# The attention output and the first token tile of the delta output turned by VectorE's blocks and a way through DRAM, in an encoder kernel of two layers

## The chip, the cores and the metric

The kernel runs on one core of one Trainium2 chip. The metric is the device time of one execution in microseconds (us), and the number compared is a median of runs. A core has a matrix engine (TensorE, PE in the profile), a vector engine (VectorE, DVE), a scalar engine (ScalarE, ACT), a general engine (GpSimd, POOL) and a sync engine (SyncE, SP) that here only issues transfers. Each works through its own queue of instructions in order, and instructions of different engines wait for one another by semaphores. PE writes its results into PSUM; the other engines bring them from there to SBUF. DMA engines move data between SBUF and DRAM.

## What is computed

Two layers of an encoder over 256 tokens with 1024 channels, in float32. Each layer projects its normalised input into the parts of two branches (a gated delta rule in both directions, and differential attention), gates the output of each branch, projects both, merges them and projects the result. The parts of the reference that matter here:

```python
def gated_delta_branch(q, k, v, ab, z, conv_w, a_log, dt_bias, norm_w):
    ...
    o = rmsnorm(o_fwd + o_bwd, norm_w.astype(f32))
    o = o.transpose(0, 2, 1, 3).reshape(bsz, seq, GDN_WIDTH).astype(z.dtype)
    return o * jax.nn.silu(z)

def diff_attention_branch(q, k, v, z, cos, sin, lam_params, subln_w, lambda_init):
    ...
    o = rmsnorm(o, subln_w) * (1.0 - lambda_init)
    o = o.transpose(0, 2, 1, 3).reshape(bsz, seq, DIFF_WIDTH)
    return o * jax.nn.silu(z)

    for l in range(DEPTH):
        h = rmsnorm(x, norm_w[l])
        proj = h @ w_in[l]
        ...
        y_a = gated_delta_branch(q_a, k_a, v_a, ab_a, z_a, ...)
        y_b = diff_attention_branch(q_b, k_b, v_b, z_b, ...)
        merged = (jax.nn.sigmoid(gate_a) * (y_a @ w_pa[l])
                  + jax.nn.sigmoid(gate_b) * (y_b @ w_pb[l]))
        x = x + merged @ w_out[l]
```

To multiply `y_a` and `y_b` by their weights, PE needs them with channels on the partitions, while they are made with tokens on the partitions. The change is about how they are turned.

## The kernel before

The 256 tokens are two tiles of 128 (m=0 and m=1), and the 1024 channels of an output are two halves of 512 (i=0 and 1), each of four heads of 128. Float32 values are multiplied as a high and a low part: for each pair of operands PE makes the products high by high (L286), high by low (L287) and low by high (L288). A token-major projection of one half (`proj_tm`) is 48 products of 128x512: eight slices `kt` of the 1024 inputs, two token tiles, three products.

The weights come in four pairs of slices per half (`weights`). Each pair is loaded by SP into `raw_*`, cast to its high part by ACT (L270, `hi_*`) and subtracted to its low part by DVE (L272, `lo_*`). `hi_*` and `lo_*` have two buffers each, so the cast of a pair waits until PE is through with the pair two before it. A name such as `lo_pb011` is layer 0, half 1, pair 1 of projection `pb`; `pp_pb000` is the PSUM bank of half 0, token tile 0.

At the end of a layer the projections run in this order: `gb` and `ga` (the two merge gates), `pb` (attention output by its weights), `pa` (delta output by its weights), then the merge (`mg`) and the output projection `o`. The output of a `pb` product is brought from PSUM by DVE with the gate (L1102). In between, the delta rule is finished by chunk stages (`chunks`, for the two groups of four heads): `y1p`, `sp`, `ks`, `y2p` and `qs`, and `po`, of 128x128 products on PE, copies on ACT and additions on DVE (the last of them L921, onto `kq`, where the delta output lies). A list of places says behind which slice of which projection each stage is issued: places 48 to 55 are the slices of `ga` half 0, 56 to 63 of `ga` half 1, 64 to 71 of `pb` half 0. A scheduler then sets the order of each engine's queue.

When the delta output is complete, ACT squares its 16 rows of heads (L1155, into `sso`), DVE and POOL make the factor `ro` (L1157, POOL's power at L157, L1159), and DVE multiplies by the factor and by the gate `za` (L1080, eight instructions for each token tile). The attention output `ob` is gated in the same way with `zb` earlier, about the time of the second half of `gb` and the first of `ga`.

The gated tiles are turned by `split_T`: four PE turns of 128x128 into a PSUM bank (L213, `pt_yb*` and `pt_ya*`), from which ACT writes the high part, scaled by the norm's weight (L222), and DVE the low part (L223) into `ybT` or `yaT`. There are four such sets of turns for each output and layer: two halves by two token tiles.

Another tile of the kernel is turned without PE already: `v` and the squares of `q` go through DVE's 32x32 block turns (L136, `tb_v`, `tb_q`), and `v` goes by POOL into a DRAM tile (L141, `bnc_v`) and back in four pieces that put the blocks in their places (L143).

## Time and profile before

| | |
|---|---|
| median of 3 runs | 758.26 us (757.37 to 758.40) |
| profiled execution | 758.15 us |
| its span, first to last instruction | 756.4 us |
| granted TensorE clock | 0.998 of full speed |
| PE, DVE, ACT, POOL busy, share of the span | 99%, 77%, 62%, 16% |
| PE turns per layer of `yb` and of `ya` | 16 and 16 |
| idle of PE put down to `lo_pa` | 0.5 us, once |

A page of the profile shows one execution on the chip. A row of a group names the line of the code, the engine, the operation, the tiles as out<-in, and then count, busy time and the idle time ahead of it with what ended it. A row of a timeline starts with its start and its duration in us; "x4" at its end joins four instructions, and square brackets hold the idle time before the first and the engine and line that ended it. PE's products overlap, so that the distance between two starts, not the duration, is what one costs. Times in the text are us in the span of the profiled execution.

### The profile page before, as it was taken

The page shows a single profiled execution, that of the slowest core. Times are in us where ns is not written, and L with a number is a line of the kernel's source. Part 1 is how long each engine was busy: PE and PEld are TensorE (multiplying, and loading weights), DVE is VectorE, ACT ScalarE, POOL GpSimd, SP SyncE. Part 2 cuts the span into 40 slices and gives each one's busy share as a digit, 9 for nine tenths or more (in the row PEclk, how much of TensorE's full clock was granted, in tenths as well). Part 3 has the DMA queues.
Part 4 walks back from the last instruction along what each step waited for, and adds up shares of the span by engine and source line. Part 5 has one row for each costly group of instructions (what it writes and reads, how often), then busy time and mean ns, then how long its engine had stood idle before and what let it go on. Part 6 is the DMA issues. An engine that isn't in the chain of part 4 may idle for free.

```text
span 756.4 us, 13840 instructions
## 1 busy us (share of the span) xinstructions
PE 745.5 (99%) x5192; PEld 642.2 (85%) x5192; DVE 581.0 (77%) x1098; ACT 471.8 (62%) x1015; POOL 121.0 (16%) x181
## 2 busy tenths in 40 slices
PE   8999999999999999999999999999999999999996
PEld 5999889977878889988889889889788888998785
DVE  7786999999886853578668779999998668436782
ACT  6657665568876675645445677565787747465552
POOL 5101431112032030100000025202111310201000
PEclk9999999999999999999999999999999999999999
DMA  8752767776677342567574258768665835336541
GB/s 261 232 167 83 229 194 206 215 217 175 202 191 178 85 120 84 168 203 240 196 230 140 84 148 258 203 187 238 181 185 183 190 114 143 104 110 207 194 140 56
DMA packets 71811, 131.26 MB, mean 174 GB/s; under 512 B 12303, under 2 KB 12767, under 8 KB 71744
## 3 DMA queue, kind: packets, MB, share of 16 engines
q1 hardware_dynamic: 64606, 113.65, 50.6%
q0 software_dynamic: 6304, 15.15, 7.5%
q10 hardware_dynamic: 834, 1.58, 0.6%
q8 instruction: 41, 0.67, 0.4%
q14 instruction: 26, 0.21, 0.1%
HBM read 123.44 MB, written 6.91 MB: 172 GB/s over the span
## 4 chain that ended last, share of the span: by engine, by line
PE 86%; DVE 7%; issue 3%; DMA 2%; ACT 2%; POOL 0%; POOLq 0%; DVEq 0%; ACTq 0%
PE pp_vb L344 4%; PE pp_qk L287 3%; PE pp_qk L288 3%; PE pp_qk L286 3%; PE pf_v L361 2%; PE pp_za L287 2%; PE pp_gb L287 2%; PE pf_v L365 2%; PE pp_gb L286 2%; PE pf_v L363 2%; PE pp_ga L286 2%; PE pp_za L286 2%; PE sc L955 2%; PE pp_za L288 2%; PE pp_gb L288 2%
## 5 line engine op out<-in xcount | busy, mean ns | idle before, releaser
L287 PE MATMUL pp_qk<-lo_qk,hT 128*128 128x512 f32 x128 | 50.9, 398 | 0.4 <-DVE lo_qk L272 0.2
L288 PE MATMUL pp_qk<-hi_qk,hT 128*128 128x512 f32 x128 | 50.0, 391 | 0.0
L272 DVE TENSOR_TENSOR lo_qk<-raw_qk,hi_qk 128x1024 fp32r<-128x1024 f32 x32 | 39.8, 1242 | 9.7 <-ACT hi_qk L270 9.3
L270 ACT CAST hi_qk<-raw_qk 128x1024 fp32r<-128x1024 f32 x28 | 29.4, 1050 | 25.3 <-PE pp_qk L288 12.6
L286 PE MATMUL pp_qk<-hi_qk,hT 128*128 128x512 f32 x128 | 45.1, 393 | 0.0
L965 ACT ACTIVATE es<-sc,mx 128x256 f32<-128x256 f32 x64 | 29.6, 473 | 19.6 <-DVE mx L963 19.6
L272 DVE TENSOR_TENSOR lo_pb<-raw_pb,hi_pb 128x1024 fp32r<-128x1024 f32 x16 | 19.6, 1226 | 23.0 <-ACT hi_pb L270 23.0
L363 PE MATMUL pf_q<-hT,hi_q 128*128 128x256 f32 x128 | 36.2, 286 | 0.0
L361 PE MATMUL pf_q<-hT,hi_q 128*128 128x256 f32 x128 | 36.1, 287 | 0.0
L361 PE MATMUL pf_v<-hT,hi_v 128*128 128x256 f32 x128 | 35.9, 285 | 0.0
L363 PE MATMUL pf_v<-hT,hi_v 128*128 128x256 f32 x128 | 35.8, 284 | 0.0
L361 PE MATMUL pf_k<-hT,hi_k 128*128 128x256 f32 x128 | 35.7, 284 | 0.0
L363 PE MATMUL pf_k<-hT,hi_k 128*128 128x256 f32 x128 | 35.7, 283 | 0.0
L272 DVE TENSOR_TENSOR lo_ga<-raw_ga,hi_ga 128x1024 fp32r<-128x1024 f32 x16 | 19.5, 1219 | 20.9 <-ACT hi_ga L270 20.9
L365 PE MATMUL pf_q<-hT,lo_q 128*128 128x256 f32 x128 | 34.8, 285 | 0.0
L365 PE MATMUL pf_v<-hT,lo_v 128*128 128x256 f32 x128 | 34.6, 288 | 0.0
L365 PE MATMUL pf_k<-hT,lo_k 128*128 128x256 f32 x128 | 34.4, 284 | 0.0
L593 DVE SCALAR_TENSOR_TENSOR cvq<-pf_q,cw,cvq 128x254 f32<-128x254 f32 (+1 forms) x64 | 29.9, 476 | 1.9 <-ACT cvq L589 1.4
L270 ACT CAST hi_pa<-raw_pa 128x1024 fp32r<-128x1024 f32 x16 | 16.8, 1053 | 22.9 <-PE pp_pa L288 16.7
L287 PEld LDWEIGHTS pp_qk<-lo_qk,hT 128*128 128x128 f32 x128 | 24.0, 188 | 7.3 <-DVE lo_qk L272 2.5
L593 DVE SCALAR_TENSOR_TENSOR cvv<-pf_v,cw,cvv 128x254 f32<-128x254 f32 (+1 forms) x64 | 30.0, 476 | 0.1
L593 DVE SCALAR_TENSOR_TENSOR cvk<-pf_k,cw,cvk 128x254 f32<-128x254 f32 (+1 forms) x64 | 28.5, 478 | 2.0 <-ACT cvk L589 1.3
(392 smaller groups left out, 2524.1 us busy)
## 6 DMA issues: line engine op xcount, KB each, us to landing
raw_qk<-in_w_in_dram SPq DMA_DIRECT2D x32, 512.0 KB, 4.0
raw_k<-in_w_in_dram SPq DMA_DIRECT2D x16, 512.0 KB, 5.3
raw_q<-in_w_in_dram SPq DMA_DIRECT2D x16, 512.0 KB, 3.7
raw_v<-in_w_in_dram SPq DMA_DIRECT2D x16, 512.0 KB, 3.8
raw_zb<-in_w_in_dram SPq DMA_DIRECT2D x16, 512.0 KB, 3.8
raw_za<-in_w_in_dram SPq DMA_DIRECT2D x16, 512.0 KB, 3.8
raw_ga<-in_w_in_dram SPq DMA_DIRECT2D x16, 512.0 KB, 4.2
raw_pb<-in_w_pb_dram SPq DMA_DIRECT2D x16, 512.0 KB, 3.8
```

Of the source, the lines that this page charges most:

```text
L270: high = (V.tensor_copy if kp in turned else S.copy)(hi[:, :, :n], raw[:, :, :n]).ins
L272: mark[nm, kp] = high, V.tensor_tensor(lo[:, :, :n], raw[:, :, :n], hi[:, :, :n].bitcast(F32), ALU.subtract).ins
L286: T.matmul(o, act[kt // 4][:, 0, kt % 4, ts_], hi, start=kt == 0, stop=False)
L287: T.matmul(o, act[kt // 4][:, 0, kt % 4, ts_], lo, start=False, stop=False)
L288: mark["proj"] = T.matmul(o, act[kt // 4][:, 1, kt % 4, ts_], hi, start=False, stop=kt == KT - 1).ins
L344: mark["proj"] = T.matmul(o, act[k_ // 4][:, pa, k_ % 4, ts_], ws[k_][1 + pw], start=k_ == 0 and n_ == 0, stop=kt == KT - 1 and n_ == len( ...
L361: T.matmul(o, hi[:, cs], act[kt // 4][:, 0, kt % 4, :], start=first, stop=False, skip_group_check=True)
L363: T.matmul(o, hi[:, cs], act[kt // 4][:, 1, kt % 4, :], start=False, stop=False, skip_group_check=True)
L365: T.matmul(o, lo[:, cs], act[kt // 4][:, 0, kt % 4, :], start=False, stop=done, skip_group_check=True)
L593: V.scalar_tensor_tensor(ca[:, o0:o1], acc[:, b, o0 + sft : o1 + sft], cw[:, j, cb : cb + 1], ca[:, o0:o1], ALU.mult, ALU.add)
L955: mm = T.matmul(sp[n][:, qt * SEQ : (qt + 1) * SEQ], qkT[h // 4][rows, 0, h % 4, qt * P : (qt + 1) * P], qkT[h // 4][rows, 1, h % 4, :], s ...
L965: S.activation(es[:, n, qt, :], spv[:, qt, :], AF.Exp, bias=mx[:, n, qt : qt + 1], accum_out=s_all[:, h, n, qt : qt + 1])
```

## The change

In the gated attention output, all four tiles of a layer, and in the gated delta output, the two tiles of m=0, the four PE turns are replaced. `send` turns a gated tile by 32x32 blocks on DVE into the buffer of the gate that it was multiplied by (`zb` or `za`), and POOL writes it to a DRAM tile `bny`. `fetch` has POOL read it back in four pieces of 64 KB, in which the blocks stand at their places. `split_B` lets ACT make the high part and DVE the low part from that buffer in SBUF, behind a named weight pair. The delta output's m=1 stays with `split_T`. The places of the chunk stages are moved from 52, 54, 57, 59, 62, 64, 67 to 52, 54, 55, 57, 58, 60, 61. Weights, products and all other stages are as before.

```diff
--- before.py
+++ after.py
@@ -221,6 +221,27 @@
         else:
             S.activation(hi, ptv, AF.Copy, scale=w)
             V.scalar_tensor_tensor(lo, ptv, w, hi.bitcast(F32), ALU.mult, ALU.subtract)
+
+    def send(tb, src, nm):
+
+        V.transpose(tb.rearrange("p j (d k) -> p j k d", k=4), src.rearrange("p k (j t) -> p j k t", j=4))
+        dd = dram.tile([4, 32, 4, P], F32, tag="bny", name=f"bny_{nm}", bufs=4)
+        mark["sent"] = G.dma_start(out=dd.rearrange("i t j x -> (i t) (j x)"),
+                                   in_=tb.rearrange("p j x -> p (j x)")).ins
+        return dd
+
+    def fetch(tb, dd, after):
+        for j in range(4):
+            with behind(after):
+                G.dma_start(out=tb[blk(j)], in_=dd[:, :, j].rearrange("i t x -> t i x"))
+
+    def split_B(dst, tb, m, w, after):
+        turned = tb.rearrange("p i (d k) -> p k (i d)", k=4)
+        hi, lo = (dst[:, part, :, m * P : (m + 1) * P] for part in range(2))
+        with behind(after[0]):
+            S.activation(hi, turned, AF.Copy, scale=w)
+        with behind(after[1]):
+            V.scalar_tensor_tensor(lo, turned, w, hi.bitcast(F32), ALU.mult, ALU.subtract)
 
     def pair(nm):
         return [big.tile([P, 2, 4, SEQ], F32R, tag="p8", name=f"{nm}_{i}", bufs=4) for i in range(2)]
@@ -1071,7 +1092,7 @@
         step(mg)
         step(mg)
 
-        def gated(o_, z_, r_, nw_, yT, nm, tiles=range(NM), after={}, halves_=range(2)):
+        def gated(o_, z_, r_, nw_, yT, nm, tiles=range(NM), after={}, halves_=range(2), sent=None):
             for i in halves_:
                 for m in tiles:
                     zv, ov = heads4(z_[i][:, m, :]), o_(i, m)
@@ -1080,7 +1101,11 @@
                             V.scalar_tensor_tensor(ov[:, j, :], ov[:, j, :],
                                                    r_[:, m, 4 * i + j : 4 * i + j + 1],
                                                    zv[:, j, :], ALU.mult, ALU.mult)
-                    split_T(yT[i], ov, m, f"{nm}{i}", w=nw_)
+                    if sent is None:
+                        split_T(yT[i], ov, m, f"{nm}{i}", w=nw_)
+                    else:
+                        tb = z_[i][:, m, :].rearrange("p (j x) -> p j x", j=4)
+                        sent[i, m] = tb, send(tb, ov, f"{nm}{i}{m}")
 
         def gate(c_base, nm, tag, between=(None, None), places=((None,) * 4,) * 2, first=(),
                  raws=({}, {})):
@@ -1117,14 +1142,18 @@
         rsqrt_rows(rb.rearrange("p q h -> p (q h)"), ssb.rearrange("p q h -> p (q h)"), 1.0 / P, 16)
         V.scalar_tensor_tensor(rb, rb, 0.5 * (1.0 - lam0), r0, ALU.mult, ALU.mult)
 
-        ybT = pair(f"ybT{l}")
+        ybT, yb_sent = pair(f"ybT{l}"), {}
         def gate_yb(i):
             at = [mark[f"ga{l}0", m][1] if i else mark[f"gb{l}1", 2 + m][1] for m in range(NM)]
             gated(lambda i, m: heads4(ob[i][:, m, :]), zb, rb, nw[:, 1:2], ybT, f"yb{l}",
-                  after={(i, m): at[m] for m in range(NM)}, halves_=(i,))
+                  after={(i, m): at[m] for m in range(NM)}, halves_=(i,), sent=yb_sent)
+            for m in range(NM):
+                fetch(*yb_sent[i, m], None)
 
         gate_yb(0)
         gta = gate(C_GA, f"ga{l}", "eo", (lambda: gate_yb(1), None))
+        for i, m in ((0, 0), (0, 1), (1, 0), (1, 1)):
+            split_B(ybT[i], yb_sent[i, m][0], m, nw[:, 1:2], mark[f"ga{l}{i}", 2 + m])
         branch(ybT, w_pb[l], gtb, f"pb{l}")
         ch = [chunks(0), chunks(1)]
 
@@ -1134,7 +1163,7 @@
                 next(gen, None)
 
         order = [(mg, 41), (mg[:1], 43), (mg[1:], 45), (mg, 48), (mg, 50)]
-        order += [(ch[i : i + 1], at + i) for at in (52, 54, 57, 59, 62, 64, 67) for i in range(2)]
+        order += [(ch[i : i + 1], at + i) for at in (52, 54, 55, 57, 58, 60, 61) for i in range(2)]
         for gens, at in order:
             if at == 52:
                 key_sums()
@@ -1149,7 +1178,7 @@
         V.tensor_tensor(rq2, rq, rq, ALU.mult)
         sso = small.tile([P, NM, NH], F32, tag="sso", name=f"sso{l}")
         ro = small.tile([P, NM, NH], F32, tag="ro", name=f"ro{l}")
-        yaT = pair(f"yaT{l}")
+        yaT, ya_sent = pair(f"yaT{l}"), {}
         for m in range(NM):
             for h in range(NH):
                 S.activation(sqj[:, :P], osb(h // 4, m)[:, h % 4, :], AF.Square,
@@ -1157,7 +1186,11 @@
             V.tensor_tensor(sso[:, m], sso[:, m], rq2[:, m], ALU.mult)
             rsqrt_rows(ro[:, m], sso[:, m], 1.0 / P, NH)
             V.scalar_tensor_tensor(ro[:, m], ro[:, m], 0.5, rq[:, m], ALU.mult, ALU.mult)
-            gated(osb, za, ro, nw[:, 0:1], yaT, f"ya{l}", (m,))
+            gated(osb, za, ro, nw[:, 0:1], yaT, f"ya{l}", (m,), sent=None if m else ya_sent)
+        for i in range(2):
+            fetch(*ya_sent[i, 0], mark["pow"])
+        for i in range(2):
+            split_B(yaT[i], ya_sent[i, 0][0], 0, nw[:, 0:1], mark[f"pb{l}1", 2 + i])
         branch(yaT, w_pa[l], gta, f"pa{l}")
 
 
```

In the changed kernel lines stand 21 further down from L225 on, and some more behind `gated`: L270 and L272 become L291 and L293, L286 to L288 become L307 to L309, L921 becomes L942, L1080 becomes L1101, L1102 becomes L1127, and L1155, L1157 and L1159 become L1184, L1186 and L1188. New are L227 (the block turn), L229 and L236 (the DMAs), L242 and L244 (`split_B`).

DVE's queue in layer 0, from the first weight pair of `pb`'s second half (`lo_pb010`) on; first before, then with the change:

```order
L1080 SCALAR_TENSOR_TENSOR kq0_344<-kq0_344,ro0_3680,za0_1_372 128x128 x4
L272 TENSOR_TENSOR lo_pb010_3133<-raw_pb010_3134,hi_pb010_3132 128x1024
L1102 SCALAR_TENSOR_TENSOR gb0_0_2743<-gb0_0_2743,pp_pb000_3054 128x512
L1157 TENSOR_TENSOR sso0_3679<-sso0_3679,rq20_3674 128x8
L1102 SCALAR_TENSOR_TENSOR gb0_0_2743<-gb0_0_2743,pp_pb001_3055 128x512
L272 TENSOR_TENSOR lo_pb011_3151<-raw_pb011_3152,hi_pb011_3150 128x1024
L223 SCALAR_TENSOR_TENSOR yaT0_0_3681<-pt_ya000_3700,nw0_291,yaT0_0_3681 128x4x128
```

```order
L293 TENSOR_TENSOR lo_pb010_3141<-raw_pb010_3142,hi_pb010_3140 128x1024
L1127 SCALAR_TENSOR_TENSOR gb0_0_2743<-gb0_0_2743,pp_pb000_3062 128x512
L1188 SCALAR_TENSOR_TENSOR ro0_3688<-ro0_3688,rq0_3683 128x8
L1127 SCALAR_TENSOR_TENSOR gb0_0_2743<-gb0_0_2743,pp_pb001_3063 128x512
L1186 TENSOR_TENSOR sso0_3687<-sso0_3687,rq20_3682 128x8
L1101 SCALAR_TENSOR_TENSOR kq0_344<-kq0_344,ro0_3688,za0_0_371 128x128 x4
L1101 SCALAR_TENSOR_TENSOR kq0_344<-kq0_344,ro0_3688,za0_1_372 128x128 x4
L293 TENSOR_TENSOR lo_pb011_3159<-raw_pb011_3160,hi_pb011_3158 128x1024
L227 STREAM_TRANSPOSE za0_0_371<-kq0_344 128x4x4x32
L1188 SCALAR_TENSOR_TENSOR ro0_3688<-ro0_3688,rq0_3683 128x8
L227 STREAM_TRANSPOSE za0_1_372<-kq0_344 128x4x4x32
L293 TENSOR_TENSOR lo_pb012_3177<-raw_pb012_3178,hi_pb012_3176 128x1024
```

The eight multiplies by the gate of m=0 (on `kq0_344`, with `za0`) stood ahead of `lo_pb010` and now stand between `lo_pb010` and `lo_pb011`, and the first block turn follows `lo_pb011`.

ACT's queue in layer 0, from the last weight pair of `pb`; before, then with the change:

```order
L270 CAST hi_pb013_3186<-raw_pb013_3188 128x1024
L222 ACTIVATE yaT0_0_3681<-pt_ya001_3735,nw0_291 128x4x128
L222 ACTIVATE yaT0_1_3682<-pt_ya011_3746,nw0_291 128x4x128
L270 CAST hi_pa000_3755<-raw_pa000_3757 128x1024
L270 CAST hi_pa001_3773<-raw_pa001_3775 128x1024
L270 CAST hi_pa002_3791<-raw_pa002_3793 128x1024
```

```order
L291 CAST hi_pb013_3194<-raw_pb013_3196 128x1024
L291 CAST hi_pa000_3767<-raw_pa000_3769 128x1024
L222 ACTIVATE yaT0_0_3689<-pt_ya001_3735,nw0_291 128x4x128
L222 ACTIVATE yaT0_1_3690<-pt_ya011_3746,nw0_291 128x4x128
L291 CAST hi_pa001_3785<-raw_pa001_3787 128x1024
L242 ACTIVATE yaT0_0_3689<-za0_0_371,nw0_291 128x4x128
L242 ACTIVATE yaT0_1_3690<-za0_1_372,nw0_291 128x4x128
L291 CAST hi_pa002_3803<-raw_pa002_3805 128x1024
```

The high parts of the turned m=0 (L242, from `za0`) stand behind the cast of the second weight pair of `pa`; L222 is now for m=1 alone.

PE's queue in layer 0, from the last product of `pb`; before, then with the change:

```order
L288 MATMUL pp_pb011_3131<-hi_pb013_3186,ybT0_1_2855 128x512
L286 MATMUL pp_pa000_3753<-hi_pa000_3755,yaT0_0_3681 128x512
L286 MATMUL pp_pa001_3754<-hi_pa000_3755,yaT0_0_3681 128x512
L287 MATMUL pp_pa000_3753<-lo_pa000_3756,yaT0_0_3681 128x512
L288 MATMUL pp_pa000_3753<-hi_pa000_3755,yaT0_0_3681 128x512
L287 MATMUL pp_pa001_3754<-lo_pa000_3756,yaT0_0_3681 128x512
L288 MATMUL pp_pa001_3754<-hi_pa000_3755,yaT0_0_3681 128x512
```

```order
L309 MATMUL pp_pb011_3139<-hi_pb013_3194,ybT0_1_2855 128x512
L307 MATMUL pp_pa000_3765<-hi_pa000_3767,yaT0_0_3689 128x512
L308 MATMUL pp_pa000_3765<-lo_pa000_3768,yaT0_0_3689 128x512
L307 MATMUL pp_pa001_3766<-hi_pa000_3767,yaT0_0_3689 128x512
L308 MATMUL pp_pa001_3766<-lo_pa000_3768,yaT0_0_3689 128x512
L309 MATMUL pp_pa001_3766<-hi_pa000_3767,yaT0_0_3689 128x512
L307 MATMUL pp_pa001_3766<-hi_pa000_3767,yaT0_0_3689 128x512
L308 MATMUL pp_pa001_3766<-lo_pa000_3768,yaT0_0_3689 128x512
L309 MATMUL pp_pa001_3766<-hi_pa000_3767,yaT0_0_3689 128x512
L307 MATMUL pp_pa001_3766<-hi_pa001_3785,yaT0_0_3689 128x512
L308 MATMUL pp_pa001_3766<-lo_pa001_3786,yaT0_0_3689 128x512
L309 MATMUL pp_pa001_3766<-hi_pa001_3785,yaT0_0_3689 128x512
```

The bank of m=0 is `pp_pa000`, that of m=1 `pp_pa001`. Both before and now the first product is of m=0; then came products of both tiles by turns, and now ten and more products of m=1 follow, up to the second weight pair, ahead of the return to m=0 (`pp_pa000` with `hi_pa000`).

## The prediction

> **What bounds the kernel now.** I read the page first: span, busy shares, the shares of the chain.
>
> ```profile
> span 756.4 us, 13840 instructions
> PE 745.5 (99%) x5192; PEld 642.2 (85%) x5192; DVE 581.0 (77%) x1098; ACT 471.8 (62%) x1015; POOL 121.0 (16%) x181
> PE 86%; DVE 7%; issue 3%; DMA 2%; ACT 2%; POOL 0%; POOLq 0%; DVEq 0%; ACTq 0%
> ```
>
> TensorE is busy for 745.5 of 756.4 us. Next I asked for busy time in two stretches of layer 0 (columns: PE, its weight loads, DVE, ACT, POOL, clock, DMA share, GB/s), from the attention output's first turns to the delta output's, and from there to the first product of `pa`.
>
> ```profile
> 256.25:320.45 64.20, 64.20 (x514) 57.46 (x513) 35.97 (x66) 40.25 (x93) 7.59 (x8) 1.00 0.42 129
> 320.45:333.18 12.73, 12.73 (x65) 10.63 (x64) 11.02 (x21) 6.54 (x8) 1.83 (x2) 1.00 0.62 205
> ```
>
> In both PE has no idle time and its clock is 1.00: a product taken off PE is time gained, unless the work that replaces it comes late. But in the second stretch DVE is busy for 11.02 of 12.73 us, so whatever is put there has almost no room.
>
> **What the change takes from PE.** Six sets of four 128x128 turns a layer leave PE: four of the attention output, two of the delta output's tile m=0. One set, between products:
>
> ```profile
> 270.31 0.60 PE L213 MATMUL pt_yb<-ident,ob 128*128 128x128 f32 x4
> 270.67 0.48 PE L287 MATMUL pp_ga<-lo_ga,hT 128*128 128x512 f32 x1
> 270.98 0.39 PE L288 MATMUL pp_ga<-hi_ga,hT 128*128 128x512 f32 x1
> 271.21 0.40 PE L287 MATMUL pp_ga<-lo_ga,hT 128*128 128x512 f32 x1
> ```
>
> A set holds PE from 270.31 to 270.67, 0.36 us; the product behind it takes 0.31 to the next start where the one after takes 0.23, 0.08 more. So 0.44 a set, 2.7 for six. The chunk stages' small products, which now stand in fewer and longer blocks, save some changes of form: two or three of the 0.08, about 0.2. Gain: 2.9 a layer, 5.8 in all.
>
> **Cost a: the weights of `pb`, second half, behind the gating on DVE.** In the order of before, only the two evacuations of `gb` stand between the low parts of the weight pairs 0 and 1 of `pb010`/`pb011`; the eight gating multiplies of m=0 were done earlier. Now the four additions of `po` end together, all squares wait for the last of them, so the gating comes late, between these two subtractions. Rows of DVE and ACT as they are now:
>
> ```profile
> 305.49 0.69 DVE L921 TENSOR_TENSOR kq<-po,kq 128x512 f32<-128x512 f32 x1 [1.46 <-PE po L919]
> 320.19 0.68 DVE L1102 SCALAR_TENSOR_TENSOR gb<-gb,pp_pb 128x512 f32<-128x512 f32 x1
> 320.79 0.16 DVE L1157 TENSOR_TENSOR sso<-sso,rq 128x8 f32<-128x8 f32 x1
> 320.87 0.68 DVE L1102 SCALAR_TENSOR_TENSOR gb<-gb,pp_pb 128x512 f32<-128x512 f32 x1
> 321.74 1.23 DVE L272 TENSOR_TENSOR lo_pb<-raw_pb,hi_pb 128x1024 fp32r<-128x1024 f32 x1 [0.19 <-ACT hi_pb L270]
> 324.21 0.15 DVE L1159 SCALAR_TENSOR_TENSOR ro<-ro,rq 128x8 f32<-128x8 f32 x1
> 324.40 2.19 DVE L1080 SCALAR_TENSOR_TENSOR kq<-kq,ro,za 128x128 f32<-128x128 f32 x8
> 308.04 0.30 ACT L1155 ACTIVATE sqj<-kq 128x128 f32<-128x128 f32 x1
> 308.46 0.31 ACT L1155 ACTIVATE sqj<-kq 128x128 f32<-128x128 f32 x1
> 308.90 0.31 ACT L1155 ACTIVATE sqj<-kq 128x128 f32<-128x128 f32 x1
> 311.74 1.03 ACT L270 CAST hi_pb<-raw_pb 128x1024 fp32r<-128x1024 f32 x1
> 322.73 0.40 PE L286 MATMUL pp_pb<-hi_pb,ybT 128*128 128x512 f32 x1
> 326.59 0.40 PE L288 MATMUL pp_pb<-hi_pb,ybT 128*128 128x512 f32 x1
> ```
>
> The two PE rows are 17 products apart: 3.86/17 = 0.227 a product, 2.73 for the 12 of a weight pair. Call E the end of the last `po` block, two products into half 0. Additions: four steps of about 0.6 (DVE's small overlap taken off its 0.69), the first result 0.35 ahead of E, so E+2.05. Squares, start to start 0.43 (308.04, 308.46, 308.90): eleven stand ahead of the cast of pair 0, 4.7; with them stand three casts at about 1.0. Its end is E+9.8, its low part (1.23) E+11.05. PE needs that after 46 products and the change of half, at about E+10.5 to 11.0: it just arrives. From there DVE has 0.60, 0.13, 0.60, 0.08 and 2.12 (the evacuations, `ro`, `sso` and the gating, start to start) and then the 1.23 of pair 1, 4.8 us, where PE has 2.73. Stall: **2.1 a layer**. Bounds: had pair 0 been early, DVE would still start at the end of `pp_pb000`, 18 products (4.1) ahead of the need; then it would want 0.43 more of waiting and 4.7, a stall of 1.05. And above, if the turns that also stand there slow down, the cost is that of the next part. I take 2.1, since the eleven squares are a counted queue.
>
> **Cost b: the start of `pa`, behind ACT and behind DRAM.** The first product of `pa` now takes the high part of tile m=0, which ACT's L242 writes from the turned tile in `za`. On ACT, L242 stands behind the cast of the second `pa` weight pair, and that cast needs the buffer which the last product of `pb` frees.
>
> ```profile
> 333.18 0.61 PE L286 MATMUL pp_pa<-hi_pa,yaT 128*128 128x512 f32 x2
> 333.38 1.06 ACT L270 CAST hi_pa<-raw_pa 128x1024 fp32r<-128x1024 f32 x1 [1.67 <-PE pp_pb L288]
> 321.61 1.25 ACT L222 ACTIVATE yaT<-pt_ya,nw 128x512 fp32r<-128x512 f32 x2
> ```
>
> With T as the end of `pb` (333.18 here): the cast starts at T+0.2 and ends at T+1.25, the copy of one tile takes about 0.7 (of 1.25 for two, overlapping), so PE waits **2.0** even if the data were long there. The wait is certain in the order; only its length is open. Queued behind L242 on ACT is the cast of pair 2, which is needed 24 products later.
>
> The data's trip: DVE turns the tile in 32x32 blocks, POOL writes it to DRAM and reads it back in four pieces. The same way exists for `v`, with these rows (the first turn for `kq`; then two POOL issues, the two DMA sizes and the spread of their landings, in us):
>
> ```profile
> 261.65 0.70 DVE L136 STREAM_TRANSPOSE tb_q<-kq 128x512 f32<-128x512 f32 x1
> 182.72 0.56 POOL L141 DMA_DIRECT2D bnc_v<-tb_v  x1 [9.67 <-DVE cc L969]
> 186.94 2.17 POOL L143 DMA_DIRECT2D tb_v<-bnc_v  x4 [3.65 <-ACT es L965]
> bnc_v<-tb_v POOLq DMA_DIRECT2D x8, 256.0 KB, 3.5
> tb_v<-bnc_v POOLq DMA_DIRECT2D x32, 64.0 KB, 3.7
> DMA to landing us min/median/max: 2.0/3.6/6.1
> ```
>
> From the write's issue to the first read's is 4.2 (182.72 to 186.94), the fourth read is issued about 1.6 later (2.17 less one 0.55), and lands 3.7 later: 9.5, and 0.7 for the turn. The first turn starts at the end of the low part of pair 1; from there PE has 34 products (7.73) and two sets of turns of m=1 (0.9), so T is 8.65 later. 0.6+4.2+1.6+3.75 = 10.2, at T+1.55, against T+1.25 at which ACT gets to it: with the 0.7 copy a stall of **2.3 a layer**. If every landing took the longest, 6.1, the trip is 2.6 and 2.4 longer, a stall of about 6.5 to 7.
>
> By the Trainium skill, "DMA: Bandwidth & Descriptors", section "Anatomy of one DMA — SWDGE (gpsimd) path", such a DMA takes about 2.0 us and its bytes over 436 GB/s: 2.6 for 256 KB and 2.15 for 64 KB as an estimate, 2.5 less than the rows over the two landings. By that the tile would be back before T, b would be its floor of 2.0, and the total 0.6 less. The medians of this trace (3.5 and 3.7) are longer than the rule, so I keep the rows.
>
> The turn with its stretched output (four words apart) has no row here; nearest is 0.70. Below that I see no gain; twice it (1.4) adds 0.7 per turn, some 1.4 to b a layer, and takes part in the range.
>
> **Cost c: a cast that waits longer.** `pa` now runs twelve products of m=1 between its first products of m=0, so pair 0 is in use until the 18th product, not the 12th, and the cast of pair 2 starts there. In layer 1 such a stall stands already:
>
> ```profile
> 707.23 1.05 ACT L270 CAST hi_pa<-raw_pa 128x1024 fp32r<-128x1024 f32 x1 [2.76 <-PE pp_pa L288]
> 708.39 0.68 PE L286 MATMUL pp_pa<-hi_pa,yaT 128*128 128x512 f32 x2
> 709.60 0.50 PE L287 MATMUL pp_pa<-lo_pa,yaT 128*128 128x512 f32 x1 [0.53 <-DVE lo_pa L272]
> ```
>
> From 708.39 two products would end at 708.85; the third starts at 709.60, 0.75 late. The same now comes in layer 0, **0.7** once, and costs nothing new in layer 1. Floor nothing, if PE's wait at the start of `pa` lets the cast catch up.
>
> **Costed at nothing.** The attention output's trip: gating ends at 249.2 and the first two turns about 1.4 later; the copies out of it stand ahead of the fourth `ga` cast, and the tiles are first read by `pb`.
>
> ```profile
> 246.99 2.19 DVE L1080 SCALAR_TENSOR_TENSOR ob<-ob,rb,zb 128x128 f32<-128x128 f32 x8
> 265.17 1.03 ACT L270 CAST hi_ga<-raw_ga 128x1024 fp32r<-128x1024 f32 x1
> 300.58 0.39 PE L286 MATMUL pp_pb<-hi_pb,ybT 128*128 128x512 f32 x1
> ```
>
> Back by about 261 against 264 on ACT; late landings would hold that cast to 266, and it has slack until its products near 270. Four turns of 0.70 on DVE lie in a stretch where it is busy for 35.97 of 64.20. POOL's added issues stand behind its last `pow` and ahead of nothing that layer needs soon. Chunk stages moved forward find their inputs by 0.6 us or more; if one doesn't, the stall is that size, once a layer.
>
> **Sum.** -5.8 + 2 x 2.1 + 2 x 2.3 + 0.7 = +3.7. The profiled execution took 758.15, 0.11 under the median of 758.26; so **761.9 us**. Floors: 758.15 - 5.8 + 2.1 + 4.0 = 758.5, with c 759.2.
>
> **Rivals.**
> *Hidden after all, so faster.* The six sets come off PE and the two waits are short; it decides where both together stay under 2.9 a layer. Fully hidden it is 758.15 - 5.8 = 752.4; half hidden about 755. For it: DVE is at 77% and ACT at 62% over the span. Against: b's 2.0 is an order on one engine, not a matter of speed, and a's eight multiplies stand in a stretch where DVE is busy for 11.02 of 12.73.
> *Slow DRAM.* All landings of the delta tile at the row's longest: b is 6.5, total 758.15 - 5.8 + 4.2 + 13.0 + 0.7 = 770.3; with half of that delay 766. For it: weights move at 205 GB/s in that stretch, more than the 129 before it, and a read is cut in pieces of 512 bytes. Against: the median of 40 such transfers is 3.6.
> *Squares in time.* If the four additions end sooner than I count, a and b are at their floors: 758.5 to 759.2, hardly to be told from no change. Against it the eleven squares.
>
> **Chances.** Forecast 0.57 (own range 760 to 765), slow DRAM 0.15, squares in time 0.18, hidden 0.10. 0.2% (1.5 us) is about what can be told from no change: "squares in time" lies inside it for two thirds, 0.12, with 0.01 of the forecast; so same 0.13, faster 0.10, slower 0.77. The range from 758 to 768 leaves out the faster case and the upper half of slow DRAM, 0.17.
>
> **What would show it.** Right: in the rows of PE a wait for `lo_pb` of about 2 in each layer, one at the first product of `pa` for `yaT` on ACT of 2 or more, ACT's L242 behind a cast that starts at `pb`'s end, and one wait on `lo_pa` in each layer; PE's busy time some 5.8 less. Wrong: L242 itself waiting on DMA by several us (slow DRAM); a `po` block or `ks` idle on ACT or DVE (the places); PE busy time hardly less; or no idle time on PE at 320 to 335.

## The result and the profile after

The changed kernel took 769.73 us (median of 4 runs, 769.18 to 770.45) against 758.12 for the kernel before in the same session: a ratio of 1.0155, 95% interval 1.0138 to 1.0173. It is slower by 11.6 us. Its profiled execution took 769.85.

First two lines of the page, then the rows of PE's waits (us in total, times, longest) at the three places that the prediction named as costs b, a and c:

```profile
span 768.1 us, 13877 instructions
PE 744.8 (97%) x5144; PEld 638.6 (83%) x5144; DVE 593.7 (77%) x1110; ACT 476.6 (62%) x1015; POOL 154.7 (20%) x241
```

```profile
PE pp_pa L307 <- ACT yaT L242: 9.1, 2, 5.0
PE pp_pb L308 <- DVE lo_pb L293: 3.2, 2, 1.6
PE pp_pa L308 <- DVE lo_pa L293: 1.1, 2, 0.5
```

PE makes 48 turns less, but its busy time is only 0.7 us less than before, not the 5.8 forecast; and it waits 13.4 us at the three places (0.5 of it, one wait on `lo_pa`, was there before). Where both come from is seen in layer 0 on PE:

```profile
321.07 0.61 PE L307 MATMUL pp_pb<-hi_pb,ybT 128*128 128x512 f32 x2
323.27 0.50 PE L308 MATMUL pp_pb<-lo_pb,ybT 128*128 128x512 f32 x1 [1.59 <-DVE lo_pb L293]
...
332.10 0.39 PE L309 MATMUL pp_pb<-hi_pb,ybT 128*128 128x512 f32 x1
337.49 0.80 PE L307 MATMUL pp_pa<-hi_pa,yaT 128*128 128x512 f32 x1 [5.00 <-ACT yaT L242]
338.09 0.63 PE L308 MATMUL pp_pa<-lo_pa,yaT 128*128 128x512 f32 x1
338.51 0.63 PE L307 MATMUL pp_pa<-hi_pa,yaT 128*128 128x512 f32 x1
...
340.91 0.40 PE L307 MATMUL pp_pa<-hi_pa,yaT 128*128 128x512 f32 x1
...
344.54 0.68 PE L307 MATMUL pp_pa<-hi_pa,yaT 128*128 128x512 f32 x2
345.74 0.50 PE L308 MATMUL pp_pa<-lo_pa,yaT 128*128 128x512 f32 x1 [0.53 <-DVE lo_pa L293]
```

At 0.227 a product, the first gap is 1.75 us too long (cost a), the second 5.16 (cost b), the last 0.75 (cost c). But between 337.49 and 340.91 stand eight products, 3.42 us where eight take 1.82: another 1.6 that the prediction doesn't have. The first of them are 0.43 apart, not 0.227, and the clock tells why (columns: PE, its weight loads, DVE, ACT, POOL, clock, DMA share, GB/s):

```profile
332.40:337.49 5.09, 0.09 (x1) 0.00 (x0) 2.47 (x5) 2.25 (x2) 0.52 (x1) 0.98 0.97 240
337.49:340.90 3.41, 3.41 (x8) 2.70 (x9) 1.50 (x2) 1.22 (x1) 0.00 (x0) 0.53 0.23 77
```

After five idle microseconds PE is granted half its clock for 3.4 us. Such products count as busy, which is why the busy time of the page hardly fell.

How the delta tile's way went, in the timelines of DVE, POOL, SP and ACT, and then its DMAs (KB each, median us to landing):

```profile
319.89 2.19 DVE L1101 SCALAR_TENSOR_TENSOR kq<-kq,ro,za 128x128 f32<-128x128 f32 x8
321.99 1.23 DVE L293 TENSOR_TENSOR lo_pb<-raw_pb,hi_pb 128x1024 fp32r<-128x1024 f32 x1
323.13 1.09 DVE L227 STREAM_TRANSPOSE za<-kq 128x512 f32<-128x512 f32 x1
...
324.52 0.64 POOL L229 DMA_DIRECT2D bny_ya<-za  x1 [2.50 <-DVE ro L1188]
328.38 2.20 POOL L236 DMA_DIRECT2D za<-bny_ya  x4 [2.38 <-DMA bny_ya<-za]
...
329.45 0.37 SPq L287 DMA_DIRECT2D raw_pa<-in_w_pa_dram  x1
331.23 0.37 SPq L287 DMA_DIRECT2D raw_pa<-in_w_pa_dram  x1
...
332.53 1.04 ACT L291 CAST hi_pa<-raw_pa 128x1024 fp32r<-128x1024 f32 x1 [1.42 <-DVE yaT L223]
336.24 1.20 ACT L242 ACTIVATE yaT<-za,nw 128x512 fp32r<-128x512 f32 x1 [2.67 <-DMA za<-bny_ya]
```

```profile
bny_ya<-za POOLq DMA_DIRECT2D x4, 256.0 KB, 3.5
za<-bny_ya POOLq DMA_DIRECT2D x16, 64.0 KB, 5.2
```

The gating stands ahead of the low part of pair 1, as the order said. ACT is free of the cast at 333.57 but has to wait for DMA until 336.24. Two loads of 512 KB are issued after the first of the reads and ahead of that wait. In layer 1 the wait at the start of `pa` is 4.06 and eight products take 3.26.

The account of the profiled execution, from starts: cost a 1.75 in each layer, 3.5; cost b 5.16 and 4.22, 9.4; slow products 1.6 and 1.44, 3.0; cost c 0.75, only in layer 0 new. Together 16.7. The turns give back 5.3 (745.5 to 740.2 busy in the run with the old places below, which has all the turns of the change and none of the waits). Of the measured 11.7 that leaves 0.3 without a place.

### The profile page after: what moved, and what is told of

It is laid out like the page before. It is cut to its first block, busy times and chain, and to the rows that moved or that the text cites. A ratio compares the mean times of both kernels' runs of the same rounds, so it can differ in the third digit from the quotient of the medians.

```text
span 768.1 us, 13877 instructions
## 1 busy us (share of the span) xinstructions
PE 744.8 (97%) x5144; PEld 638.6 (83%) x5144; DVE 593.7 (77%) x1110; ACT 476.6 (62%) x1015; POOL 154.7 (20%) x241
## 3 DMA queue, kind: packets, MB, share of 16 engines
q10 hardware_dynamic: 834, 1.58, 0.6%
## 4 chain that ended last, share of the span: by engine, by line
PE 75%; DVE 11%; issue 4%; DMA 4%; ACT 4%; POOL 1%; POOLq 0%; DVEq 0%; SPq 0%; ACTq 0%
PE pp_vb L365 5%; PE pp_qk L308 2%; PE pp_qk L309 2%; PE pp_qk L307 2%; PE pp_za L308 2%; PE pf_v L382 2%; PE pf_k L386 2%; PE pf_v L386 2%; PE pp_gb L308 2%; PE pp_gb L307 2%; PE pf_k L384 2%; PE pf_v L384 2%; PE pf_k L382 2%; PE pp_pa L308 2%; PE pp_ga L307 2%
## 5 line engine op out<-in xcount | busy, mean ns | idle before, releaser
L309 PE MATMUL pp_qk<-hi_qk,hT 128*128 128x512 f32 x128 | 50.0, 391 | 0.0
L293 DVE TENSOR_TENSOR lo_qk<-raw_qk,hi_qk 128x1024 fp32r<-128x1024 f32 x32 | 39.6, 1239 | 9.6 <-ACT hi_qk L291 9.1
L307 PE MATMUL pp_qk<-hi_qk,hT 128*128 128x512 f32 x128 | 45.1, 393 | 0.0
L291 ACT CAST hi_qk<-raw_qk 128x1024 fp32r<-128x1024 f32 x28 | 29.4, 1048 | 24.2 <-PE pp_qk L309 11.5
L293 DVE TENSOR_TENSOR lo_pb<-raw_pb,hi_pb 128x1024 fp32r<-128x1024 f32 x16 | 19.5, 1221 | 29.1 <-ACT hi_pb L291 29.1
L307 PE MATMUL pp_pa<-hi_pa,yaT 128*128 128x512 f32 x64 | 24.9, 419 | 9.1 <-ACT yaT L242 9.1
L291 ACT CAST hi_pa<-raw_pa 128x1024 fp32r<-128x1024 f32 x16 | 16.8, 1049 | 24.1 <-PE pp_pa L309 17.3
```

What stands on the lines that cost most here:

```text
L291: high = (V.tensor_copy if kp in turned else S.copy)(hi[:, :, :n], raw[:, :, :n]).ins
L293: mark[nm, kp] = high, V.tensor_tensor(lo[:, :, :n], raw[:, :, :n], hi[:, :, :n].bitcast(F32), ALU.subtract).ins
L307: T.matmul(o, act[kt // 4][:, 0, kt % 4, ts_], hi, start=kt == 0, stop=False)
L309: mark["proj"] = T.matmul(o, act[kt // 4][:, 1, kt % 4, ts_], hi, start=False, stop=kt == KT - 1).ins
```

## The experiments

Every kernel is the changed one but for what is named. The kernel before took 757.96 to 758.6 beside them.

**Parts alone.** The places of the chunk stages without any turn by DRAM: `sent` is left out of both calls of `gated`, and with it the `fetch` and `split_B` of both outputs.

> The kernel with the changed places of the chunk stages alone: all turns by PE as before, nothing by DRAM. Theory (the loss is made by the delta tile's way through DRAM): 757.5 to 759.5 us, no wait on yaT at the start of pa, and at most 1 us of waits on lo_pb. Rival (the tighter places themselves make the squares and the gating late): a wait on lo_pb of 1.6 to 2 in each layer, 761 to 763 us.

Measured 757.67 (ratio to the kernel before 0.9994, interval 0.9984 to 1.0003), no wait on `lo_pb` or `yaT` among PE's waits. The places alone are harmless.

The attention output alone, old places:

```diff
-        order += [(ch[i : i + 1], at + i) for at in (52, 54, 55, 57, 58, 60, 61) for i in range(2)]
+        order += [(ch[i : i + 1], at + i) for at in (52, 54, 57, 59, 62, 64, 67) for i in range(2)]
...
-            gated(osb, za, ro, nw[:, 0:1], yaT, f"ya{l}", (m,), sent=None if m else ya_sent)
-        for i in range(2):
-            fetch(*ya_sent[i, 0], mark["pow"])
-        for i in range(2):
-            split_B(yaT[i], ya_sent[i, 0][0], 0, nw[:, 0:1], mark[f"pb{l}1", 2 + i])
+            gated(osb, za, ro, nw[:, 0:1], yaT, f"ya{l}", (m,))
```

> The attention output alone by blocks and DRAM, the delta output by PE, the old places. Theory (this half of the change is covered, and eight sets of PE turns at 0.44 are gained): 754.6 us, 754 to 755.5, PE without new waits. Rival (the copies out of the turned tile, 1.2 us on ACT and 1.1 on DVE in the trace of the change where they took 0.7, hold up the casts of ga): a wait on lo_ga or hi_ga of 0.5 or more in each layer, and 757 us or more.

Measured 753.65 (0.9937, 0.9922 to 0.9952). PE is busy for 741.6, 3.9 less than before: 0.49 for each of eight sets, where 0.44 was worked out. The copies do take 1.24 and 1.13, but no cast of `ga` shows in PE's waits.

The whole change with the old places, one line:

```diff
-        order += [(ch[i : i + 1], at + i) for at in (52, 54, 55, 57, 58, 60, 61) for i in range(2)]
+        order += [(ch[i : i + 1], at + i) for at in (52, 54, 57, 59, 62, 64, 67) for i in range(2)]
```

> The whole change, but with the old places. Theory (the place of the gating decides: with it ahead of the first weight pair of pb's second half, cost a goes, 3.7, and the trip starts some 5 us earlier): no wait on lo_pb, a wait for yaT of 0 to 2.5 a layer and no slow products behind it, 753 to 759, most likely 756. Rival (the trip takes so long under the weight loads that it comes late from anywhere): a wait of 4 or more at the start of pa in each layer with slow products behind, 763 to 766.

Measured 752.23 (0.9917, 0.9901 to 0.9934). That is below the range I gave and 17.5 below the change: with the old places the turns taken off PE are worth their full price. The window that holds most of `pb`'s second half (columns as above), and the timelines of DVE, POOL and ACT:

```profile
318.00:330.00 12.00, 12.00 (x58) 9.75 (x57) 10.33 (x20) 7.00 (x13) 6.81 (x11) 1.00 0.91 279
```

```profile
315.63 1.09 DVE L227 STREAM_TRANSPOSE za<-kq 128x512 f32<-128x512 f32 x1
318.08 1.20 DVE L293 TENSOR_TENSOR lo_pb<-raw_pb,hi_pb 128x1024 fp32r<-128x1024 f32 x1
...
321.94 4.44 POOL L236 DMA_DIRECT2D za<-bny_ya  x8
...
329.24 1.24 ACT L242 ACTIVATE yaT<-za,nw 128x512 fp32r<-128x512 f32 x1
```

PE is never idle there. The block turn starts at 315.63, 7.5 us earlier than in the change and ahead of the low part of pair 0; the reads start 6.4 earlier, and the copy waits for nothing.

**One number of the table.** Two kernels put back the places of both `po` stages (52, 54, 55, 57, 58, 64, 67), or of the last alone (52, 54, 55, 57, 58, 60, 67).

> The whole change with the places of the two po stages alone put back (52, 54, 55, 57, 58, 64, 67). In this program's order the po additions are apart again, tile m=0 first, the gating of m=0 and its block turns stand ahead of the first weight pair of pb's second half. Theory (the one cause of the loss is that the four additions came together, and with them late squares, gating and turns): 752 to 753, no wait on lo_pb or yaT. Rival (the closer stages of y1p to qs cost by themselves when the attention output's copies stand on ACT): 755 or more.

> The whole change with the place of the last po stage alone put back (52, 54, 55, 57, 58, 60, 67). The additions of m=0 stand together and ahead, those of m=1 apart behind the fourth weight pair of pb's first half. Theory: as for the two stages put back, 752 to 753, so that one number of the table carries the whole loss. Rival: part of it stays, 755 or more, with a wait on lo_pb or yaT.

Measured 752.15 (0.9922, 0.9904 to 0.9940) and 752.03 (0.9922, 0.9906 to 0.9937). A single number, 61 or 67, carries the whole difference of 17.7 us. With 67 the additions of m=0 come first and alone, and from there on the order is that of the old places:

```profile
305.07 1.29 DVE L942 TENSOR_TENSOR kq<-po,kq 128x512 f32<-128x512 f32 x2 [0.55 <-PE po L940]
...
315.72 1.09 DVE L227 STREAM_TRANSPOSE za<-kq 128x512 f32<-128x512 f32 x1
```

In the change all four additions stand together, and the one that the first squares read, of the first four heads and m=0, is the last of them. DVE and ACT there:

```profile
307.41 2.48 DVE L942 TENSOR_TENSOR kq<-po,kq 128x512 f32<-128x512 f32 x4 [3.68 <-PE po L940]
...
309.99 0.31 ACT L1184 ACTIVATE sqj<-kq 128x128 f32<-128x128 f32 x1 [7.01 <-DVE kq L942]
```

ACT stood idle for 7 us, and the sixteen squares came after that instead of in between. That is what makes the gating, and with it the block turns, late.

**Which half meets the places.** The new places with the attention output alone by DRAM, and with the delta tile alone.

> The new places with the attention output alone by DRAM; all of the delta output is turned by PE. In this program's order the four additions of po stand together and the gating of m=0 stands between the weight pairs of pb's second half, as in the full change. Theory (cost a comes from the meeting of the new places with the attention output's way, b from the delta tile alone): the wait on lo_pb of 1.6 in each layer, nothing on L242 at the start of pa; against the same half with the old places (753.65) 1.8 to 2 a layer more, 757 to 758. Rival (the late chunk stages cost nothing without the delta tile's trip): 753.5 to 754.5.

> The new places with the delta tile m=0 alone by DRAM; the attention output is turned by PE. In this program's order the gating of m=0 stands two weight pairs earlier than in the full change. Theory (the trip is harmless when it starts early): no wait on lo_pb or yaT, the gain of four sets of PE turns at 0.44, 1.8, on the time of the places alone (757.67): 755 to 756.5. Rival (the delta tile's trip is late with the new places in any case): a wait on yaT of 2 or more a layer, 760 or more.

The first: 755.43 (0.996, 0.9947 to 0.9973), 1.8 above the same half with the old places. The expected wait came at half its size, 0.7 a layer, because eight PE turns now stand in the gap:

```profile
321.59 1.03 PE L213 MATMUL pt_ya<-ident,kq 128*128 128x128 f32 x8
323.31 0.50 PE L308 MATMUL pp_pb<-lo_pb,ybT 128*128 128x512 f32 x1 [0.69 <-DVE lo_pb L293]
```

Without them (0.89) PE would be as late as in the change (an estimate: 0.69 and 0.89 are 1.58, against 1.59). In this run the four additions stand together (from 307.44); with the places alone and with the delta tile alone the first of them starts at 300.6 and 300.8, 5.6 ahead of the next. So it is the attention output's way, with the close places, that makes the four additions meet in the schedule (by which of its copies was not tried), and taking PE's turns out of that stretch also takes out what covered DVE.

The second was a miss: 766.02 (1.0111, 1.0088 to 1.0134), where 755 to 756.5 was expected of a trip that starts early. PE's waits there are many small ones:

```profile
PE pp_pb L308 <- DVE lo_pb L293: 2.6, 4, 0.8
PE pp_pa L307 <- ACT yaT L242: 2.3, 1, 2.3
PE pp_pa L308 <- DVE lo_pa L293: 1.7, 3, 0.6
```

The same window as above:

```profile
318.00:330.00 12.00, 11.20 (x52) 8.76 (x51) 9.73 (x18) 4.79 (x6) 9.12 (x12) 1.00 1.03 335
```

The DMA engines are full, 1.03 at 335 GB/s, against 0.91 at 279 with the old places. POOL's sends stand ahead of its second `pow`, which starts at 320.10 and takes 2.74 where it took 1.64 in the change, and DVE waits 0.83 for it. The sends need not be the reason for the length: with the places alone, where nothing is sent, the same `pow` took 2.61. Which of these waits makes the loss of this half was not tried apart.

I then put the last `po` place back in this kernel too (67 for 61), to see whether the same number heals it.

> The delta tile m=0 alone by DRAM, the attention output by PE, and the new places with the last po stage alone put back (67 for 61). In this program's order both sends stand ahead of POOL's second pow's input, the additions of m=1 stand behind the block turn, and L242 stands behind the cast of pa's first weight pair instead of ahead of it. Theory (the 8 us that the delta tile alone lost with the new places come from m=1's work meeting the trip, which the same number removes): 755 to 756.5, no wait on lo_pb or yaT. Rival (they come from the DMA engines being full at that moment, which the place doesn't change): 760 or more, with a DMA share near 1 from 318 to 330.

Measured 764.05 (1.0081, 1.0059 to 1.0102): not healed. The DMA share from 318 to 330 is 0.96, but PE is not idle there, and layer 0 shows no wait for `yaT`. The loss is in layer 1, on ACT and PE:

```profile
704.90 1.22 ACT L242 ACTIVATE yaT<-za,nw 128x512 fp32r<-128x512 f32 x1 [1.18 <-DMA za<-bny_ya]
...
706.18 0.80 PE L307 MATMUL pp_pa<-hi_pa,yaT 128*128 128x512 f32 x1 [3.84 <-ACT yaT L242]
```

There L242 stands, as in the full change, behind the cast of `pa`'s second weight pair (701.50 to 702.56) and two copies of m=1, and the data is late besides. The twelve products behind take 5.28 us where twelve take 2.72, at a clock of 0.50. PE's waits in layer 1 (3.84, 0.88 on `lo_pb`, 0.53 on `lo_pa`) and the 2.56 lost by these products make 7.8, which is what the profiled execution (763.70) lost against the 755.9 that the places alone less 1.8 would give. So the number 67 repairs the order only together with the attention output's way; with PE turning the attention output the schedule of layer 1 comes out as bad again. The DMA engines are not full there (0.68 from 694 to 706); how much their traffic adds was not tried apart.

**What b is made of.** First the clock: 22 products between `pb` and `pa`, of the length of PE's wait; their result is not used.

```diff
+        idle = bank(f"idle{l}")
+        for n_ in range(22):
+            with behind(mark["done", f"pb{l}1", KT - 1]):
+                T.matmul(idle, ybT[0][:, 0, 0, :P], ybT[1][:, 0, 0:2, :].rearrange("p k t -> p (k t)"),
+                         start=True, stop=True)
         branch(yaT, w_pa[l], gta, f"pa{l}")
```

> The whole change, with 22 products in each layer between pb and pa whose result is not used, about 5.0 us, as long as PE's wait there. Theory (the products of 0.43 us behind the wait come from PE's idleness, by which the granted clock falls to half): the products behind are 0.23 apart at once, the copy L242 starts as late as before, and the time falls by 2.5 to 3, to 767. Rival (the slow products come from elsewhere, the transfers or the copies of that moment): they stay at 0.43 and the time at 769.7 or above.

Measured 766.81, 2.9 less than the change, by doing more work:

```profile
332.55 5.15 PE L1197 MATMUL idle<-ybT,ybT 128*128 128x512 f32 x22
337.94 0.50 PE L307 MATMUL pp_pa<-hi_pa,yaT 128*128 128x512 f32 x1 [0.24 <-ACT yaT L242]
338.28 0.40 PE L308 MATMUL pp_pa<-lo_pa,yaT 128*128 128x512 f32 x1
```

The data is as late as before (the copy starts 4.1 us behind `pb`'s end, 3.9 in the change); the products behind are 0.23 apart, in both layers. The 3.0 us of slow products come from PE's idleness.

Then the reads. Two loads of `pa`'s first half are held back until the copy L242, which is what `mark["copied"]` names:

```diff
-        branch(yaT, w_pa[l], gta, f"pa{l}")
+        branch(yaT, w_pa[l], gta, f"pa{l}", held={2: mark["copied"], 3: mark["copied"]})
```

> The whole change, but the loads of the third and fourth weight pair of pa's first half are issued by ACT behind the copy L242, not by SP during the trip. Theory (the pieces read from DRAM share the DMA engines with two weight loads of 512 KB, DMA share 0.97 to 0.99): pieces of za land in 3.5 to 4 instead of 5.2, the wait at the start of pa falls from 5.0 and 4.1 to about 3, with the clock's loss smaller too; a new wait for the held weights of up to 2 comes later, so the total is open, 766 to 770. Rival (512-byte pieces are slow by themselves): landing at 5 or more, the wait at the start of pa unchanged.

Measured 765.21 (1.0085, 1.0069 to 1.0102), 4.5 less than the change and a little below the range expected. Its DMA row, then the timelines of ACT and PE in layer 0, then PE and the clock in layer 1:

```profile
za<-bny_ya POOLq DMA_DIRECT2D x16, 64.0 KB, 2.3
```

```profile
332.69 0.39 PE L309 MATMUL pp_pb<-hi_pb,ybT 128*128 128x512 f32 x1
334.07 1.21 ACT L242 ACTIVATE yaT<-za,nw 128x512 fp32r<-128x512 f32 x1
335.34 0.50 PE L307 MATMUL pp_pa<-hi_pa,yaT 128*128 128x512 f32 x1 [2.25 <-ACT yaT L242]
...
343.12 1.05 ACT L291 CAST hi_pa<-raw_pa 128x1024 fp32r<-128x1024 f32 x1 [2.31 <-DMA raw_pa<-in_w_pa_dram]
```

```profile
708.59 0.50 PE L307 MATMUL pp_pa<-hi_pa,yaT 128*128 128x512 f32 x1 [2.26 <-ACT yaT L242]
```

```profile
709.74:713.15 3.41, 3.41 (x10) 2.63 (x9) 1.10 (x1) 0.00 (x0) 0.00 (x0) 0.50 0.99 348
```

The pieces land in 2.3 instead of 5.2, and the copy L242 waits for nothing: the 2.25 that PE still waits is the time of the cast and the copy alone. In layer 0 the products behind are at full clock. In layer 1 they are not, although the wait is the same: from 709.74, 1.15 us behind the first of them, the clock is halved for 3.41 us, and nine products take 3.65 where nine take 2.04. The held weights then come 2.3 late on ACT in layer 0, and PE waits there once more on `lo_pa`, 0.5 by the starts, which gives part of it back. The Trainium skill, "DMA: Bandwidth & Descriptors", section "Anatomy of one DMA — SWDGE (gpsimd) path", has a fit by which, as an estimate, 64 KB take 2.15: this run is near it, and the change is 3 away from it, with the weight loads beside the reads.

Last the words' distance. The turn writes, and the copies read, words side by side; the tokens of a turned tile are then in another order than the product needs.

```diff
-        V.transpose(tb.rearrange("p j (d k) -> p j k d", k=4), src.rearrange("p k (j t) -> p j k t", j=4))
+        V.transpose(tb.rearrange("p j (k d) -> p j k d", k=4), src.rearrange("p k (j t) -> p j k t", j=4))
...
-        turned = tb.rearrange("p i (d k) -> p k (i d)", k=4)
+        turned = tb.rearrange("p i x -> p (i x)").rearrange("p (k y) -> p k y", k=4)
```

> The whole change, but the turn writes its words side by side and the copies read them side by side; the tokens of a turned tile are then in another order than the product needs. Theory (words four apart cost the turn 1.09 instead of 0.70, the copies 1.21 and 1.14 instead of 0.69 and 0.74): L227 0.70, L242 0.69 or less, L244 0.74 or less; in each layer the trip starts 0.4 sooner and the copy ends 0.5 sooner, so the wait at the start of pa is 0.9 shorter, and the time 767.5 to 768.3. Rival (the price comes from reading and writing while the DMA engines are busy): the durations stay, and the time too, 769.7.

Groups of this run (xcount | busy, mean ns):

```profile
L244 DVE SCALAR_TENSOR_TENSOR ybT<-zb,nw,ybT 128x512 fp32r<-128x512 f32 x8 | 5.9, 737 | 0.0
L227 DVE STREAM_TRANSPOSE zb<-ob 128x512 f32<-128x512 f32 x8 | 5.4, 688 | 0.1
...
L242 ACT ACTIVATE ybT<-zb,nw 128x512 fp32r<-128x512 f32 x8 | 5.8, 722 | 0.0
```

The durations are as the theory said: 0.69, 0.72 and 0.74, against 1.09, 1.23 and 1.13 in the change. PE's wait at the start of `pa` fell from 9.1 to 7.7. The time, 769.97 (1.0149, 1.0131 to 1.0166), cannot be told from the change's: ten products took 3.98 in each layer where ten take 2.27 (337.12 to 341.10 in layer 0), which takes back 0.4 of the 1.3 that the waits are shorter by the starts, and the rest is within the spread of these runs (768.29 to 771.08). Settled for the durations, not for the time.

**Too early.** A third table, 52, 54, 57, 59, 62, 63, 64.

> The whole change with the places 52, 54, 57, 59, 62, 63, 64: early stages as of old, po in between. In this program's order the block turns of m=0 stand one weight pair earlier than with the old places, the gating of m=1 stands between the first two pairs of pb's second half, and the copy L242 stands ahead of the last weight cast of pb. Theory (work of the length of the gating between these two pairs makes a wait, whichever tile it is of, and a copy that stands on ACT ahead of its data holds the casts behind it): a wait on lo_pb of 0.5 to 1.6 a layer and casts held by L242, 755 to 764. Rival (only the start of the trip counts, and it is earlier): 752 to 753.

Measured 761.94 (1.0054, 1.0038 to 1.0070). The tile is turned earliest of all, and yet:

```profile
PE pp_pb L308 <- DVE lo_pb L293: 3.6, 6, 0.7
PE pp_pb L307 <- ACT hi_pb L291: 3.3, 2, 1.6
```

```profile
328.91 1.20 ACT L242 ACTIVATE yaT<-za,nw 128x512 fp32r<-128x512 f32 x1 [4.35 <-DMA za<-bny_ya]
```

The schedule put L242 ahead of the last cast of `pb`, ACT waited 4.35 for the data, and the cast behind it came late. Behind the two waits of layer 0 (1.64 and 0.65) the clock is halved from 332.69 to 336.10; behind the same two in layer 1 it is not. A start of the trip decides nothing by itself; the copy's place in ACT's queue against its data does.

## Why the prediction was wrong

Forecast 761.9, range 758 to 768; measured 769.73. The sign and the three places were right, and two terms were not.

*Gain.* -5.8 forecast, -5.3 measured in PE's busy time. Right, though six sets at 0.44 are 2.64 and not 2.7.

*Cost a.* "Stall: **2.1 a layer**"; measured 1.75. Right: the eight multiplies stand between the two weight pairs, and E, the squares and the casts came as counted. The eight turns that the change takes from PE there were a cover for it, which I had counted only as a gain.

*Cost b.* The "stall of **2.3 a layer**" failed; it was 5.16 and 4.22. This is 4.8 of the 7.8 us by which the forecast was short, and the missing term below is 3.0; the other terms nearly cancel. The order was right, that ACT gets to L242 at T+1.25; the floor of 2.0 should have been 2.4 (in the run with held loads 335.34 - 332.69 - 0.23), since the copy takes 1.2 and not "about 0.7": I gave it the row of L222, which reads PSUM side by side, not words four apart. The trip failed mostly at one link. "The fourth read is issued about 1.6 later, and lands 3.7 later": the issue was right, the landing was 6.2 (the fourth read is issued at 328.38 + 2.20 - 0.55 = 330.03, the copy starts at 336.24). I took the median of rows from another stretch. Those of this stretch share the engines with the loads of `pa`'s weights, and the row that I put down to the rival, 205 GB/s, was the one to work from. With the loads held, the landing was 2.3; that the stall is then 2.25, the number forecast, is chance, since it is there the floor with the longer copy and not the end of the trip. The other links were off by less, and partly against one another: from the turn's start to the write's issue it took 1.4 (323.13 to 324.52), not 0.6, and from the write's issue to the first read's 3.9, not 4.2. The 4.2 came from a row whose wait ended on ACT (L965) and not on the write. `pb` ended 9.2 behind the turn's start, not 8.65.

*The missing term.* 3.0 us of slow products, put at nothing without a word. The step from a late tile to a halved clock was not in any case of mine. It was not safe to leave out even at the stall of 2.3 that I forecast: of the five idle times of about that size ahead of products of `pb` and `pa` in these runs (two of them pairs of waits, 1.64 and 0.65), two were followed by slow products, and of the five from 3.5 to 5.0 all were.

*Cost c.* 0.7 in layer 0, measured 0.75. Right.

*Rivals.* "Slow DRAM" was right on the reads, which landed in 6.2 where it took the row's longest, 6.1, and wrong on the write, behind whose issue the first read went out after 3.9, no later than forecast. That its 770.3 is so near the measured time is luck: it has it by a wait of 6.5 that was not there and without the slow products, and its own terms (2.25 and 2.6 and 2.4) make a wait of 7.25, about 772. Two of the signs that I had named for a wrong forecast were there: L242 waiting on DMA (2.67), and PE's busy time hardly less.

"Hidden after all" gave 752.4. It is what the turns are worth with one place put back, 752.03; I had seen in the order that the additions stood together, and not asked whether the table of places did that rather than the turns.

## What to carry to other kernels

When a change takes work off the engine that bounds and moves a schedule as well, run the two apart: here the turns give 5.7 us with the old places, the places alone nothing, and both together lose 11.6; and one place decides only with its neighbours as they are, as the delta tile alone showed. A round trip through DRAM on a critical path is priced by the transfers that share its moment, not by the median of the same transfer elsewhere. And a wait of PE of 2.3 us can cost, and each of 3.5 or more did cost here, another 1.4 to 2.6 by the clock.

## What the runs showed of the hardware

PE's clock: behind waits of 3.52, 3.84, 4.06, 4.21 and 5.00 us the granted clock was 0.50 each time, and 128x512 products stood 0.43 apart; it cost 1.71, 2.56, 1.44, 1.71 and 1.60. Behind shorter ones it went either way: waits of 2.25 (held loads, layer 0) and 2.31 (delta tile alone) left products 0.23 apart, and one of 2.26 (held loads, layer 1) was followed by half the clock and cost 1.6. In the run with the third table the pair of waits of 1.64 and 0.65 cost 1.7 in layer 0, and the same pair nothing in layer 1. The half clock lasted 3.41 each time, and 6.83 behind the wait of 3.84. It began while PE was still waiting or up to 1.15 us after its first product, so the length of the wait alone does not decide. The Trainium skill, "TensorE: Matmul & The Clock Gate", section "What's actually happening", names about 3.4 us for both, of idleness to halve the clock and of work to restore it; the trace agrees on the length of the half clock, but not that it takes an idleness of 3.4, and there the measurement decides.

Words 16 bytes apart in SBUF cost more than half again on both engines: 0.69 to 1.09 for DVE's block turn of 128x512, 0.72 to 1.23 for ACT's copy, 0.74 to 1.13 for DVE's.

POOL's `pow` on 128x8 (L157) took 1.64 to 1.66 us, behind a send as well as without one, but for three times in these traces: 2.74 (delta tile alone), 2.61 (places alone, where nothing is sent) and 1.92 (delta tile alone with the number 67). Those three, and no others, started while DVE was in the subtraction of a weight pair (L293): 1.21, 1.11 and 0.39 of it were left, and the `pow` was 1.10, 0.97 and 0.28 longer. No run tried this by itself.
